# A network of ten stages on one core: expert weights in 2 MB slots with 16 KB per partition, and two more megabytes loaded before the expert stage

## The chip, the cores and the metric

The kernel runs on one core of one Trainium2 chip. It is one program that computes three network blocks one after the other. The metric is the device time of one execution in microseconds, as the median of several runs. All matrices are float32.

## The reference, cut to what matters

The change touches only the mixture of experts in the second block. There are 256 tokens of width 1024 and 32 experts; each token goes to four of them. Cut to the arithmetic, an expert does this with its tokens:

```python
gu = xb @ w1[e] + b1[e]                       # 1024 -> 2048
gate = jnp.minimum(gu[:, :D_FF_2], SWIGLU_LIMIT)
up = jnp.clip(gu[:, D_FF_2:], -SWIGLU_LIMIT, SWIGLU_LIMIT)
act = (up + 1.0) * gate * jax.nn.sigmoid(SWIGLU_ALPHA * gate)
return (act @ w2[e] + b2[e]) * g[:, None]     # 1024 -> 1024
```

`w1` is `w_expert_in_2`, 8 MB an expert, and `w2` is `w_expert_out_2`, 4 MB an expert. Thirty-two experts are 384 MB of weights, more than half of the 721 MB that the whole program moves. Every expert's weights are read once.

## The kernel before

The expert stage is `moe_body`. It runs from about 685 us to 1692 us of the trace. It works through 16 pairs of experts (`pair`, L1697), the two experts side by side: a matmul has up to 64 tokens of one expert as its stationary side and fills half of the PE array's columns, and the other expert's matmul fills the other half. In one pair, PE does these things in order: four products with `w_expert_in` (two column halves `c`, each with a gate and an up `part`; tile `xg` holds the gathered tokens), and between and behind them the gated activation on DVE and ACT (`gm`, `um`), transposed into `aT`; then two products with `w_expert_out` (`c` = 0, 1), each copied to `ye` by ACT and added to the tokens' sums by four matmuls `ogT,ye`. Matmuls `oh,hh` and `oh,hl` gather the next pair's tokens into a bank, from which ACT copies `xg`; they are placed among the products of the current pair. A pair ends with its second `ogT,ye` group.

So a pair has six groups of weights, o0 to o5, of 4 MB each: 2 MB of either expert. Before the change a group is four loads of 1 MB, in the order lower half of the rows of expert 0, of expert 1, upper half of expert 0, of expert 1. Each load is one contiguous megabyte in memory, 8 KB for each of 128 partitions. `slot` (L1526) takes the buffers in rotation: eight 1 MB buffers of the pool `ring2` (tag `raw2`), then four of `self.ring` (tag `raw`), which all stages share. A load can be issued when PE has done the last matmul with what its buffer held before.

All of these loads are issued by SP, in order. If one waits for its buffer, everything behind it on SP waits too. The hardware's queue holds what was issued already; eight completion lanes (DMAHW0 to DMAHW7 in the order's rows) are used in turn, and a load also waits for the previous one of its lane.

Two further things share the stage. Before it, during the memory attention, `prefetch` loads the first 15 MB of pair 0: twelve into the ring, and three (`SPARE`, group indices 4, 13, 14) into buffers that are idle then. These loads stand on SP among those of `w_mem_q` and `w_mem_o`. And in pairs 3 to 6 (`FILL` = 3), PE does a product for the next block with 1 MB of `l_mem_wkv`, the fill: 48 matmuls. The fill's megabyte takes a buffer of tag `raw` at the end of the pair before, is split there by ACT (CAST to `whi`) and DVE (`wlo`), and its buffer is free when the split is done. The source of that product, `mem_3`, is loaded by GpSimd at the start of the stage into a buffer of its own (`kv0`), and its norm is worked out after pair 1.

After pair 7 stands a loop for experts with more than 64 tokens (`more`, L1785); here it runs zero rounds, but all engines pass through its branch.

The order of instructions on each engine is not written out. A planner goes through the code with modelled times of engines and loads, and decides from them what goes next: where the gather's matmuls are placed among a product's, and where the fill's split stands on ACT and DVE. When the sizes and waits of the loads change, that order changes too.

## Time and profile before

| | |
|---|---|
| median of three runs | 2866.47 us (2864.63 to 2870.25) |
| the profiled execution, its own time | 2866.68 us |
| its span in the trace | 2864.9 us |
| expert stage in the trace | about 685 to 1692 us |
| PE busy over the span | 96% |
| DMA over the whole span | 721 MB, mean 252 GB/s |

The median and the profiled execution differ by 0.2 us. Outside the expert stage, the DMA engines are about half busy. Inside it they move 421 GB/s in most slices, while PE's busy share is 94% and more. PE's busy time is modelled from pipelined matmuls, so a high share alone doesn't tell whether PE or the loads set the pace. That is read from the stretches of one pair: the length of a pair from end to end, the DMA share in it, and what PE waits for.

### The profile page before, as it was taken

Reading aid. Unit: us, or ns where it says so; the run is one execution under the profiler, and the core shown is the slowest. Engines: PE = TensorE matmul, PEld = TensorE weight load, DVE = VectorE, ACT = ScalarE, POOL = GpSimd, SP = SyncE. Lnnn points to the kernel's source line nnn. Section 1 sums busy time; section 2 is a strip of 40 time slices with the busy share of each in tenths; the row PEclk is TensorE's granted clock in tenths of the full one; section 3 lists DMA queues with packets and bytes.
Section 4 is the critical chain, followed back from the end, with each engine's and each line's share of the span. In section 5 each row is a group of like instructions: output and inputs, shape, how many; then the busy total and the mean of one; then the engine's idle time right before and its main releaser. Section 6 shows DMA issues by size and latency. Waiting matters only on the chain.

```text
span 2864.9 us, 45348 instructions
## 1 busy us (share of the span) xinstructions
PE 2751.9 (96%) x19079; PEld 2166.1 (76%) x19079; DVE 1340.0 (47%) x2203; ACT 1081.8 (38%) x1770; POOL 88.0 (3%) x153
## 2 busy tenths in 40 slices
PE   7999999999999999899999999999999999999999
PEld 7899999997434444333334359999899989999999
DVE  5566877564111111111101145569765555676655
ACT  4454655653011111000000034456654444566543
POOL 0000000010000000000000000001100000000000
PEclk9999999999999999999999999999999999999999
DMA  8446555475998999899999987654445585654453
GB/s 214 139 154 198 191 177 177 148 264 216 379 405 362 371 370 421 363 421 421 421 421 421 421 294 198 200 160 147 135 148 181 173 207 188 193 164 146 149 180 130
DMA packets 305638, 721.16 MB, mean 252 GB/s; under 512 B 13925, under 2 KB 233493, under 8 KB 256402
## 3 DMA queue, kind: packets, MB, share of 16 engines
q1 hardware_dynamic: 302194, 707.85, 67.0%
q0 software_dynamic: 2944, 10.08, 2.5%
q8 instruction: 152, 2.49, 0.4%
q14 instruction: 60, 0.49, 0.0%
q10 hardware_dynamic: 288, 0.25, 0.0%
HBM read 710.00 MB, written 8.13 MB: 251 GB/s over the span
## 4 chain that ended last, share of the span: by engine, by line
PE 49%; DVE 4%; ACT 2%; DMA 2%; issue 1%; ACTq 0%; DVEq 0%
PE bank L115 49%; DMA raw<-l_ffn_wd 2%; DVE wlo L115 1%; ACT whi L115 1%; DVE um L115 1%; DVE att_s L115 1%; DVE xnl L115 1%; ACT xnh L115 0%; ACT att_s L115 0%; ACT ye L115 0%; DVE att_nm L115 0%; DVE xT L115 0%; ACT sq L115 0%; ACT ma_p L115 0%; DVE rs_t L115 0%
## 5 line engine op out<-in xcount | busy, mean ns | idle before, releaser
L115 DVE TENSOR_TENSOR wlo<-raw,whi 128x1024 fp32r<-128x1024 f32 x560 | 687.4, 1230 | 534.5 <-ACT whi L115 531.3
L115 PE MATMUL bank<-xnh,whi 128*128 128x256 f32 x2960 | 847.3, 287 | 6.8 <-ACT xnh L115 6.8
L115 PE MATMUL bank<-xnl,whi 128*128 128x256 f32 x2960 | 842.1, 285 | 6.8 <-DVE xnl L115 6.8
L115 PE MATMUL bank<-xnh,wlo 128*128 128x256 f32 x2960 | 839.3, 284 | 2.2 <-DVE wlo L115 2.2
L115 ACT CAST whi<-raw 128x1024 fp32r<-128x1024 f32 x560 | 584.0, 1046 | 678.5 <-PE bank L115 618.8
L115 PEld LDWEIGHTS bank<-xnh,whi 128*128 128x128 f32 x2960 | 568.7, 192 | 14.9 <-ACT xnh L115 6.8
L115 PEld LDWEIGHTS bank<-xnl,whi 128*128 128x128 f32 x2960 | 568.9, 192 | 11.7 <-DVE xnl L115 10.9
L115 PEld LDWEIGHTS bank<-xnh,wlo 128*128 128x128 f32 x2960 | 568.9, 192 | 3.0 <-DVE wlo L115 2.8
L115 PE MATMUL bank<-raw,xg 128*64 128x512 f32 x2024 | 476.6, 595 | 9.7 <-DMA raw<-w_expert_in 9.6
L115 PEld LDWEIGHTS bank<-raw,xg 128*64 128x64 f32 x2024 | 162.2, 137 | 291.1 <-issue 267.9
L115 PE MATMUL bank<-hh,whi 128*128 128x256 f32 x880 | 248.9, 284 | 10.8 <-ACT whi L115 10.8
L115 PE MATMUL bank<-raw,aT 128*64 128x512 f32 x1024 | 254.1, 597 | 0.7 <-ACT aT L115 0.7
L115 PE MATMUL bank<-hh,wlo 128*128 128x256 f32 x880 | 249.8, 284 | 0.9 <-DVE wlo L115 0.9
L115 PE MATMUL bank<-hl,whi 128*128 128x256 f32 x880 | 250.0, 284 | 0.2 <-DVE hl L115 0.2
L115 PEld LDWEIGHTS bank<-hh,whi 128*128 128x128 f32 x880 | 169.0, 193 | 11.2 <-ACT whi L115 11.2
L115 PEld LDWEIGHTS bank<-raw,aT 128*64 128x64 f32 x1024 | 75.7, 136 | 130.7 <-issue 126.6
L115 PEld LDWEIGHTS bank<-hh,wlo 128*128 128x128 f32 x880 | 169.4, 193 | 1.5 <-DVE wlo L115 1.5
L115 PEld LDWEIGHTS bank<-hl,whi 128*128 128x128 f32 x880 | 169.6, 193 | 0.6 <-DVE hl L115 0.6
L115 PE MATMUL bank<-whi,xnh 128*128 128x256 f32 x544 | 160.4, 295 | 7.1 <-ACT whi L115 7.1
L115 PE MATMUL bank<-wlo,xnh 128*128 128x256 f32 x544 | 155.9, 287 | 2.8 <-DVE wlo L115 2.8
L115 PE MATMUL bank<-whi,xnl 128*128 128x256 f32 x544 | 155.6, 286 | 0.5 <-DVE xnl L115 0.5
L115 DVE TENSOR_SCALAR gm<-bank 128x512 f32<-128x512 f32 x32 | 22.1, 692 | 261.4 <-PE bank L115 261.4
(379 smaller groups left out, 2689.1 us busy)
## 6 DMA issues: line engine op xcount, KB each, us to landing
raw<-w_expert_in SPq DMA_DIRECT2D x253, 1024.0 KB, 17.9
raw<-w_expert_out SPq DMA_DIRECT2D x128, 1024.0 KB, 16.9
raw<-l_ffn_wg SPq DMA_DIRECT2D x44, 1024.0 KB, 5.4
raw<-l_ffn_wu SPq DMA_DIRECT2D x44, 1024.0 KB, 5.4
raw<-l_ffn_wd SPq DMA_DIRECT2D x44, 1024.0 KB, 4.9
raw<-w_in SPq DMA_DIRECT2D x32, 1024.0 KB, 5.3
raw<-l_w_in SPq DMA_DIRECT2D x26, 1024.0 KB, 5.2
raw<-w_up SPq DMA_DIRECT2D x22, 1024.0 KB, 5.1
```

Of the source, the lines that this page charges most:

```text
L115: return real(*a, **k)
```

## The change

An expert's part of a group, 2 MB, becomes one load with 16 KB for each partition (`whole`). `ring2` now has four buffers of 2 MB in place of eight of 1 MB, so the room is the same. Two groups of three go there. Every third group is loaded as four halves of 1 MB (`half`) into the four shared `raw` buffers; a half reads 8 KB out of each partition's 16 KB. The weights lie in memory in another order (`layout`), made beforehand: each expert's part is contiguous, 16 KB a partition. A group is asked for once, at its first half of the rows (`get`), and both experts' loads of 2 MB must have landed before its first matmul.

`prefetch` loads 17 MB instead of 15. The two further megabytes go into a buffer `extra` in the stage's work pool, and into the buffer of `mem_3`, which is free until then; the load of `mem_3` moves behind pair 0, still on GpSimd's queue. What remains of o4 is loaded in the stage (`rest`).

```diff
--- before.py
+++ after.py
@@ -307,8 +307,7 @@
     pass
 
 
-RING2 = 8
-SPARE = (4, 13, 14)
+RING2 = 4
 LOOP = 7
 FILL = 3
 MIXAT = 5
@@ -1513,8 +1512,6 @@
         es, pool, ring2 = st.moe_es, st.moe_pool, st.ring2
         st.kv_es = ExitStack()
         st.kv0.own = nc.pool(st.kv_es, name="kv0")
-        st.kv0.raw = st.kv0.own.tile([128, KB, T], F32, tag="kv0", name="mem0")
-        nc.gpsimd.dma_start(out=st.kv0.raw, in_=A["mem_3"].rearrange("(k p) t -> p k t", p=128))
         wk = nc.pool(es, 1, name="moew", side="right")
         st.kv0.pool = Instead(wk, hn_q="gm", hn_q2="um", hn_ms="hn_ms")
         new = lambda name, shape, dt=F32: pool.tile(shape, dt, name=name)
@@ -1523,19 +1520,28 @@
         WI, WO = A["w_expert_in_2"], A["w_expert_out_2"]
         self.slots = 0
 
-        def slot(W):
-
-            p, tag = (self.ring, "raw") if self.slots % (4 + RING2) >= RING2 else (ring2, "raw2")
-            self.slots += 1
-            t = p.tile([128, 4, 512], F32, tag=tag, name=tag)
+        def half(W, pool=self.ring, tag="raw"):
+
+            t = pool.tile([128, 4, 512], F32, tag=tag, name=tag)
             nc.sync.dma_start(out=t, in_=W)
             return [t[:, k] for k in range(4)]
 
-        def spare(W, whole):
-            if whole:
-                t = self.ops.tile([128, 4, 512], F32, tag="xnl", name="spare")
-                nc.sync.dma_start(out=t, in_=W)
-                return [t[:, k] for k in range(4)]
+        def whole(W, k0=0):
+
+            t = ring2.tile([128, KB, 512], F32, tag="raw2", name="raw2")
+            nc.sync.dma_start(out=t[:, k0:], in_=W[:, k0:])
+            return [t[:, k] for k in range(KB)]
+
+        def slot(Ws):
+
+            self.slots += 1
+            if self.slots % 3:
+                return [whole(W) for W in Ws]
+            a = [half(W[:, :4]) for W in Ws]
+            b = [half(W[:, 4:]) for W in Ws]
+            return [a[e] + b[e] for e in range(2)]
+
+        def spare(W):
             r = []
             for k, tag in ((0, "whi"), (2, "wlo")):
                 t = self.wsp.tile([128, 2, 512], F32, tag=tag, name="spare")
@@ -1556,13 +1562,25 @@
         def order(n):
 
             es = (2 * n, 2 * n + 1)
-            return ([WI[e, 2 * part + c, kh] for c in range(2) for part in range(2) for kh in range(2) for e in es]
-                    + [WO[e, c, kh] for c in range(2) for kh in range(2) for e in es])
+            return [[WI[e, 2 * part + c] for e in es] for c in range(2) for part in range(2)] + [
+                [WO[e, c] for e in es] for c in range(2)]
 
         def prefetch(n):
 
-            for i, W in enumerate(order(n)[:4 + RING2 + len(SPARE)]):
-                ahead.append(spare(W, i == SPARE[0]) if i in SPARE else slot(W))
+            o = order(n)
+            for i in range(3):
+                ahead.append(slot(o[i]))
+            a, b = o[3]
+            b0 = half(b[:, :4], wk, "extra")
+            c0 = half(o[4][0][:, :4], st.kv0.own, "kv0")
+            a0 = half(a[:, :4], self.ops, "xnl")
+            a1, b1 = spare(a[:, 4:]), spare(b[:, 4:])
+            ahead.append([a0 + a1, b0 + b1])
+
+            def rest():
+                self.slots += 1
+                return [c0 + whole(o[4][0], 4)[4:], whole(o[4][1])]
+            ahead.append(rest)
 
         prefetch(0)
 
@@ -1700,7 +1718,15 @@
             if fill:
                 self.issue(fill)
             og, xg = next(got)
-            get = over_slot if over else lambda W, e: ahead.pop(0) if ahead else slot(W)
+            got2 = []
+
+            def get(Ws, kh):
+                if over:
+                    return [over_slot(W[:, 4 * kh:4 * kh + 4], e) for e, W in enumerate(Ws)]
+                if kh == 0:
+                    w = ahead.pop(0) if ahead else slot(Ws)
+                    got2[:] = w() if callable(w) else w
+                return [w[4 * kh:4 * kh + 4] for w in got2]
             aT, ye = ((self.ops, "xnl"), (self.ops, "xnh")) if over else ((self.wsp, "whi"), (self.wsp, "wlo"))
             aT = aT[0].tile([128, KB, 128], F32, tag=aT[1], name="aT")
             late = []
@@ -1720,7 +1746,7 @@
                     bk = begun.pop(0) if begun else biased(n, c, part)
                     bks.append(bk)
                     for kh in range(2):
-                        w = [get(WI[e0 + e, 2 * part + c, kh], e) for e in range(2)]
+                        w = get([WI[e0 + e, 2 * part + c] for e in range(2)], kh)
                         for k in range(4):
                             for e in range(2):
                                 mm(out=bk[64 * e:64 * e + 64, :], lhsT=xg[:, 4 * kh + k, e], rhs=w[e][k],
@@ -1767,7 +1793,7 @@
             for c in range(2):
                 bk = self.bank()
                 for kh in range(2):
-                    w = [get(WO[e0 + e, c, kh], e) for e in range(2)]
+                    w = get([WO[e0 + e, c] for e in range(2)], kh)
                     for k in range(4):
                         for e in range(2):
                             mm(out=bk[64 * e:64 * e + 64, :], lhsT=aT[:, 4 * kh + k, 64 * e:64 * e + 64],
@@ -1810,6 +1836,10 @@
             done = pair(i, got.pop(i), y, between=None if i in (LOOP, 15) else lambda: prepare(i + 1),
                         fill=st.kv0.order[i - FILL] if FILL <= i < FILL + 4 else None)
             yield NOW
+            if i == 0:
+                kv = st.kv0
+                kv.raw = kv.own.tile([128, KB, T], F32, tag="kv0", name="mem0")
+                nc.gpsimd.dma_start(out=kv.raw, in_=A["mem_3"].rearrange("(k p) t -> p k t", p=128))
             if i == LOOP:
                 more()
                 prepare(i + 1)
@@ -2286,7 +2316,7 @@
         a = np.asarray(inputs[name])
         a = a if a.ndim == 2 else a[0]
         if name in ("w_expert_in_2", "w_expert_out_2"):
-            a = a.reshape(32, 2, 4, 128, -1, 512).transpose(0, 4, 1, 3, 2, 5)
+            a = a.reshape(32, 8, 128, -1, 512).transpose(0, 3, 2, 1, 4)
         arrays[name] = f(a)
     return arrays
```

The first place is on SP at the end of a pair ahead of a fill: the pair's last expert loads, the fill (`l0_mem_wkv`), and the next pair's first loads. Names in brackets are the counters that a load waits for: load lanes (DMAHW), or the engine that last used the buffer. Before:

```order
L115 DMA raw_8414<-w_expert_out_2 128x2048 [waits DMAHW2_49,PE_49]
L115 DMA raw_8446<-l0_mem_wkv_3 128x8x256 [waits DMAHW3_49,PE_49]
L115 DMA raw_8499<-w_expert_in_2 128x2048 [waits DMAHW4_49,PE_49]
L115 DMA raw_8501<-w_expert_in_2 128x2048 [waits DMAHW5_49,PE_49]
L115 DMA raw_8511<-w_expert_in_2 128x2048 [waits DMAHW6_49,DMAHW2_49,PE_49]
L115 DMA raw2_8513<-w_expert_in_2 128x2048 [waits DMAHW7_49]
...
L115 DMA raw_8588<-w_expert_in_2 128x2048 [waits DMAHW7_49,DVE_49]
```

After:

```order
L115 DMA raw2_8358<-w_expert_out_2 128x4096 [waits DMAHW2_49,PE_49]
L115 DMA raw2_8360<-w_expert_out_2 128x4096 [waits DMAHW3_49,PE_49]
L115 DMA raw_8400<-l0_mem_wkv_3 128x8x256 [waits DMAHW4_49,PE_49]
L115 DMA raw_8453<-w_expert_in_2 128x2048 [waits DMAHW5_49,PE_49]
L115 DMA raw_8455<-w_expert_in_2 128x2048 [waits DMAHW6_49,PE_49]
L115 DMA raw_8457<-w_expert_in_2 128x2048 [waits DMAHW7_49,PE_49]
L115 DMA raw_8459<-w_expert_in_2 128x2048 [waits DMAHW4_49,DMAHW0_49,DVE_49]
L115 DMA raw2_8480<-w_expert_in_2 128x4096 [waits DMAHW1_49,PE_49]
L115 DMA raw2_8482<-w_expert_in_2 128x4096 [waits DMAHW2_49,PE_49]
```

Before, two 1 MB loads follow the fill, and the third waits for PE's use of the pair's last load (lane DMAHW2), with eight loads behind it. After, three 1 MB loads follow it, and the fourth waits for DVE's use of the fill's own megabyte (lane DMAHW4).

The second place is on ACT at the same end of the pair, from the pair's first `ye` copy to its last `xg` copies; `whi` is the fill's split. Before:

```order
L115 COPY ye_8694<-bank_8695 128x512 [waits PE_49]
L115 COPY xg_8761<-bank_8762 128x256 [waits PE_49,Activation_49]
L115 COPY ye_8694<-bank_8725 128x512 [waits PE_49]
L115 CAST whi_8866<-raw_8755 128x1024 [waits DMAHW4_49]
L115 CAST whi_8870<-raw_8755 128x1024
L115 COPY xg_8761<-bank_8772 128x256 [waits PE_49]
```

After:

```order
L115 COPY ye_8640<-bank_8641 128x512 [waits PE_49]
L115 COPY xg_8699<-bank_8700 128x256 [waits PE_49,Activation_49]
L115 COPY xg_8699<-bank_8710 128x256 [waits PE_49]
L115 CAST whi_8800<-raw_8693 128x1024 [waits DMAHW5_49]
L115 CAST whi_8804<-raw_8693 128x1024
L115 COPY ye_8640<-bank_8667 128x512 [waits PE_49]
L115 COPY xg_8699<-bank_8720 128x256 [waits PE_49]
```

The split moved ahead of the second `ye` copy, and behind a second `xg` copy.

The third place is on PE in pair 13, the second `w_expert_out` group, from the first `ogT,ye` group to the second. Before:

```order
L115 MATMUL bank<-ogT,ye 128x256 x4
L115 MATMUL bank<-oh,hh 128x128
...
L115 MATMUL bank<-oh,hh 128x128
L115 MATMUL bank<-raw_16202,aT 64x512
L115 MATMUL bank<-raw_16200,aT 64x512
...
L115 MATMUL bank<-raw_16202,aT 64x512
L115 MATMUL bank<-oh,hl 128x128
L115 MATMUL bank<-oh,hh 128x128
L115 MATMUL bank<-raw_16212,aT 64x512
L115 MATMUL bank<-oh,hl 128x128
```

After:

```order
L115 MATMUL bank<-ogT,ye 128x256 x4
L115 MATMUL bank<-oh,hh 128x128
...
L115 MATMUL bank<-oh,hl 128x128
L115 MATMUL bank<-oh,hh 128x128
L115 MATMUL bank<-raw_15984,aT 64x512
L115 MATMUL bank<-raw_15982,aT 64x512
...
L115 MATMUL bank<-raw_15984,aT 64x512
L115 MATMUL bank<-oh,hl 128x128
...
L115 MATMUL bank<-ogT,ye 128x256 x4
```

Before, the gather's matmuls stand as 3, 2, 10 and 4 among weight matmuls in runs of 7, 1 and 7. After, 17 of them stand together ahead of a run of 15 weight matmuls, and 4 behind it. The same change of order is in pairs 2 and 8 to 14.

## Rows read from the trace of the kernel before

**Rows 1.** Windows by pair: us, busy time (instructions) by engine, PEclk, DMA share, GB/s.

```profile
870.00:938.00 68.00, 62.08 (x309) 29.06 (x307) 9.96 (x16) 10.04 (x16) 0.00 (x0) 1.00 0.94 386
...
1333.00:1393.00 60.00, 56.85 (x268) 23.66 (x267) 6.84 (x13) 4.94 (x10) 0.00 (x0) 1.00 1.01 421
```

**Rows 2.** PE's timeline at pair ends 2, 6, 8, 14: start, us, engine, operation.

```profile
868.10 1.99 PE L115 MATMUL bank<-ogT,ye 128*128 128x256 f32 x8
...
1140.96 1.99 PE L115 MATMUL bank<-ogT,ye 128*128 128x256 f32 x8
...
1270.93 1.99 PE L115 MATMUL bank<-ogT,ye 128*128 128x256 f32 x8
...
1631.15 1.99 PE L115 MATMUL bank<-ogT,ye 128*128 128x256 f32 x8
```

**Rows 3.** PE's waits, 871 to 1143: engine, line <- awaited: us, times, longest.

```profile
PE bank L115 <- DVE um L115: 11.5, 8, 1.6
PE bank L115 <- DMA raw<-w_expert_in: 9.6, 9, 1.3
```

**Rows 4.** PE's waits, 685 to 871, the longest of five rows.

```profile
PE bank L115 <- DVE um L115: 2.4, 2, 1.6
```

**Rows 5.** PE's waits, 1274 to 1692, the longer of two rows.

```profile
PE bank L115 <- DVE um L115: 16.7, 14, 1.6
```

**Rows 6.** Tile whi, 900 to 925: count, ns min/median/max, first and last start.

```profile
L115 PE MATMUL bank<-whi,xnl x16: 279/283/283, 911.9 to 917.3; 128*128 128x256 f32 x16
```

**Rows 7.** SP's timeline around the end of pair 2 (two windows).

```profile
841.15 7.03 SPq L115 DMA_DIRECT2D raw<-w_expert_in  x2
...
867.45 5.04 SPq L115 DMA_DIRECT2D raw<-w_expert_in  x9
```

**Rows 8.** Windows at the ends of pairs 2 to 5, columns as in rows 1.

```profile
855.00:870.00 15.00, 14.92 (x74) 8.33 (x72) 0.81 (x5) 5.29 (x9) 0.00 (x0) 1.00 0.24 87
930.00:940.00 10.00, 9.92 (x58) 6.16 (x55) 2.36 (x2) 3.59 (x6) 0.00 (x0) 1.00 0.48 190
1000.00:1010.00 10.00, 9.92 (x55) 6.03 (x56) 2.85 (x4) 3.97 (x7) 0.00 (x0) 1.00 0.55 208
1070.00:1075.00 5.00, 4.92 (x25) 3.00 (x21) 1.06 (x1) 2.75 (x4) 0.00 (x0) 1.00 0.30 108
```

**Rows 9.** Timeline of ACT and DVE at the end of pair 2.

```profile
867.46 0.59 ACT L115 COPY ye<-bank 128x512 f32<-128x512 f32 x1 [3.98 <-PE bank L115]
...
869.63 2.00 ACT L115 CAST whi<-raw 128x1024 fp32r<-128x1024 f32 x2
...
870.71 2.36 DVE L115 TENSOR_TENSOR wlo<-raw,whi 128x1024 fp32r<-128x1024 f32 x2 [10.73 <-ACT whi L115]
```

**Rows 10.** PE's timeline, second half of pair 10.

```profile
1370.51 7.09 PE L115 MATMUL bank<-raw,aT 128*64 128x512 f32 x32
...
1379.91 0.41 PE L115 MATMUL bank<-oh,hh 128*128 128x128 f32 x1
...
1384.42 1.07 PE L115 MATMUL bank<-raw,aT 128*64 128x512 f32 x2
1385.42 0.33 PE L115 MATMUL bank<-oh,hl 128*128 128x128 f32 x1
...
1386.68 3.65 PE L115 MATMUL bank<-raw,aT 128*64 128x512 f32 x14
...
1391.01 1.35 PE L115 MATMUL bank<-ogT,ye 128*128 128x256 f32 x5
```

**Rows 11.** DMA queue 1 in 1275 to 1650: packets, MB, share of 16 engines.

```profile
q1 hardware_dynamic: 21643, 157.59, 101.1%
```

**Rows 12.** The same in 1700 to 2800, after the expert stage.

```profile
q1 hardware_dynamic: 143852, 182.64, 51.3%
```

**Rows 13.** Window 727 to 762 in pairs 0 and 1, columns as in rows 1.

```profile
727.00:762.00 35.00, 34.92 (x171) 17.84 (x171) 2.32 (x7) 3.25 (x7) 0.00 (x0) 1.00 0.82 334
```

**Rows 14.** PE's waits, 585 to 690, all rows.

```profile
PE bank L115 <- DVE xnl L115: 0.6, 2, 0.3
```

## The prediction, made before the changed kernel ran

> **What bounds the kernel now.** Only the expert stage changes, so I read that stage and leave the rest of the time alone. First come the windows, one for each pair of experts. In a pair with no extra product the DMA engines are full (share 1.01, 421 GB/s) and PE is busy 56.85 of 60 us; in a pair with a fill (a 1 MB load of the next network's weights and its product) the DMA share is 0.94, in a longer stretch [rows 1]. The starts of the last ogT group of the pairs give the period: 868.10 to 1140.96 is four fill pairs, 68.2 us each; 1270.93 to 1631.15 is six pairs of 60.04 us [rows 2]. Then the list of waits, by engine. PE waits for weights only in the fill pairs: 9.6 us in nine waits [rows 3]; before them its list has five rows, from pair 8 on two (the longer of these: 14 waits for DVE), and all are short waits for DVE and ACT [rows 4, 5]. So the steady pairs are bound twice: PE's own order takes 60.04 us and the DMA queue is full for the same time. One that gets faster alone brings nothing. As a check on the 9.6: the product is sixteen triples of matmuls, whose last ones start from 911.9 to 917.3, 0.36 us apart: 5.8 us [rows 6]; 60.04 + 5.8 = 65.8, and four pairs at 68.2 are 9.6 us over that.
>
> Where these 9.6 us come from is seen on SP. The fill takes one of four raw buffers, so the fourth raw load after it (counting it) must wait until PE has used the last megabyte of the pair. SP issues two loads at 841.15, then nothing more goes out until 867.45, when nine come in a burst [rows 7]. The queue runs dry meanwhile: DMA share 0.24 in 855-870, 0.48 in 930-940, 0.55 in 1000-1010, 0.30 in 1070-1075 [rows 8]. That is 11.4 + 5.2 + 4.5 + 3.5 = 24.6 us of idle DMA.
>
> **Term A, the wait behind the fill: -7.5 us.** The change leaves the four-buffer ring to the halved groups alone. After the fill come three halves whose buffers were used a group and more earlier, and only the fourth waits, now for the fill's split (CAST on ACT, wlo on DVE) instead of the pair's last matmul. Two things follow. One more megabyte is queued ahead of the wait: 1.049 MB at 421 GB/s is 2.49 us. And the split now stands before the pair's last ye copy on ACT; before, ye started at 867.46 and the CASTs at 869.63 [rows 9]. In the changed order the split can begin when the gather's first two xg copies are done, with 15 matmuls of the last group still to run, 7.1 us by a run of 32 records (16 matmuls) in the trace [rows 10]; two CASTs in 2.00 us and the second wlo behind them (two in 2.36 us) end some 3.4 us later, so the buffer comes free about 3.5 us sooner than the last matmul did. Together 6.0 us. Taken from the four stretches: 11.4 - 6.0 = 5.4 us remain, the other three vanish; 19.2 of 24.6 us, or 78%, and 78% of 9.6 us is 7.5. Bounds: 0 (the wait only changes its name) and 9.6 (no wait left). The freed PE time is not taken back by DMA: 25 MB per fill pair at 2.49 us are 62.3 us, under PE's 65.8.
>
> **Term B, the steady pairs: -3.9 us.** Two effects, of which the smaller counts.
> PE's order: in the last WO group the gather for the next pair no longer cuts the weights' run into 7, 1 and 7 matmuls; it stands in one piece ahead of a run of 15. Experts share the array by column halves, and a run that stops on the odd one leaves a half unused: one record pair alone takes 1.00 us (1384.42 to 1385.42). From the first gather to ogT the stretch is 11.1 us now (1379.91 to 1391.01) [rows 10]. The new order has 21 gather matmuls there at 0.126 us (ten took 1385.42 to 1386.68) and 15 weight matmuls, at most 7.1 us: 9.75 us. PE saves about 1.3 us a pair, bounds 1.0 and 1.6.
> DMA: two thirds of the bytes go in 16 KB runs. The trace has no run that long. Queue 1 has 21643 packets for 157.59 MB at 101.1% of 375 us on 16 engines, 280 ns for 7281 B [rows 11]; after the expert stage it has 143852 packets for 182.64 MB at 51.3% of 1100 us, 62.8 ns for 1270 B [rows 12]. A line through the two gives 17 ns a packet and 0.0362 ns a byte: two packets of 8 KB 627 ns, one of 16 KB 610, 2.7% less. Sixteen of a pair's 24 MB are 39.8 us, so 1.1 us at most; the other bound is nothing (the bytes themselves may be the limit). I take the middle, 0.55, because the line joins packets of mixed sizes and is extended beyond its end. PE's 1.3 us covers it. Seven pairs (8 to 14; 15 gathers nothing, so its order on PE is as before) make 3.9 us, bounds 0 and 7.7.
> The Trainium skill, "DMA: Bandwidth & Descriptors", section "Why small descriptors are slow", puts a fixed 3 cycles on a packet that moves 32 B a cycle: 259 cycles for 8 KB, 515 for 16 KB, a gain of 0.6% and not 2.7%. By it term B would be an estimated 1.6 us.
>
> **Term C, PE's order elsewhere: -2.5 us.** Pair 2 has the same rearrangement and no wait for DMA [rows 4]: 1.3 us. Pairs 1 and 3 to 6 lose one break between kinds of matmul each. The middle piece's surplus over a full slot (1.00 against 7.1/8 = 0.89) is 0.1 us and a gather run's start costs about as much; 0.25 us each, 1.2 in all. Bounds 1 and 3.
>
> **Edits costed at nothing.** The two further megabytes before the stage land earlier, but PE waits for no weights before 871 [rows 4], and the ring fills up anyway: in 727-762 the DMA share is 0.82, 6.3 us idle [rows 13]. More data ahead is only more idle time later. If the queue were the bound, they would be worth 2 x 2.49 = 5.0 us; I keep that as an end. mem_3's load now falls between pairs 0 and 1, in the same idle time; it is needed after pair 1, some 50 us later; without that cover it costs 2.5 us. The 2 MB loads that stand between those of w_mem_q and w_mem_o put up to one megabyte more ahead of two of them, 2.5 us each if uncovered; but PE's only wait in 585-690 is 0.6 us for DVE [rows 14]. At the end, both experts' 2 MB must have landed before the last 16 matmuls, not the last half: 3.5 us at most, if DMA were last there. SP's fewer issues free no one.
>
> **Sum.** 7.5 + 3.9 + 2.5 = 13.9 us. The profiled execution took 2866.68 us (span 2864.9), 0.2 above the median of the runs: 2852.8, say 2853.
>
> **Rivals.**
> (1) Nothing moves. The wait on the split lasts as long as that on the last matmul, since the split cannot start before its load has landed and ACT is in order; and 16 KB runs gain nothing. Term C alone remains, perhaps 1 to 3 us more: 2861 to 2866. For it: ACT's CAST must still pass the xg copies, whose PE work is at the end of the pair. Against it: the extra megabyte in the queue alone covers half of three of the four stretches.
> (2) The queue is the bound all through, and all is credited: 9.6 + 7.7 + 3 + 5 = 25.3 us, 2841. For it: DMA share 1.01 in the steady pairs. Against: PE without any wait for DMA there [rows 5].
> (3) Slower, by coarser pieces. Before, PE starts a group when the first 2 of its 4 MB are there and uses them in 3.5 us while the rest lands; now both experts' full 2 MB must be there. Wherever PE has caught up with DMA, the group ends up to 3.5 us later. Place: after each of the four fill breaks, at the loop after pair 7 and in every pair if the stage is paced by DMA. Price: five places are 17.5 us, which with term C and without A and B is 2866.7 + 17.5 - 2.5 = 2882. It decides as soon as weights land less than 3.5 us before use; with three such places A and C are eaten up. The trace speaks against it in the steady pairs (no wait for a load in 418 us), for it in the fill pairs, which do wait.
>
> **How the numbers follow.** Forecast 0.60; rival 1 0.16; rival 2 0.10; rival 3 0.14. A measurement of this kernel tells some 0.2% (5.7 us) from no change. Faster by more than that: 0.60 + 0.10 = 0.70; within: 0.16; slower: 0.14. The range runs from 2841 (rival 2) to 2869 (rival 1 and the mildest of rival 3), leaving out most of rival 3 and a little below.
>
> **What would show it.** A: SP's blocked stretch at the ends of pairs 2 to 5 short, the DMA share there near 1 (some idle left at the first), PE's 9.6 us of waits down to 2 and a fill pair at 66 us. B: steady pairs at 59.5 us with a DMA rate of 423 to 427 GB/s and one run of 15 matmuls; at 60.0 with 421 GB/s, long runs gain nothing; at 58.7, DMA was not the bound. C: pair 2 at 61.8. Wrong would be: PE waits for raw2 loads in steady pairs (rival 3), a rate below 421 GB/s (each percent costs 0.6 us a pair), or changes outside the expert stage.

## The result: 2846.5 us, 19 us less, and the profile after

| | before | after |
|---|---|---|
| median | 2865.55 us | 2846.52 us (2845.49 to 2851.73, 4 runs) |
| ratio of the runs | | 0.9934, 95% interval 0.9923 to 0.9946 |
| profiled execution, span | 2864.9 us | 2849.9 us |

Timed again, beside the experiments, the changed kernel took 2849.43 us, ratio 0.9942 (0.9926 to 0.9957). The profiled execution is the longest of the first four runs, so its span shows 15.0 us of the 19.0.

The windows by pair, of the changed kernel (columns as in rows 1). They answer to [rows 1]; both kinds of pair are shorter, so the windows are.

```profile
868.00:934.00 66.00, 63.53 (x326) 30.18 (x324) 9.21 (x15) 9.53 (x17) 0.00 (x0) 1.00 1.00 414
...
1320.00:1379.00 59.00, 55.85 (x270) 23.57 (x268) 6.84 (x13) 5.03 (x10) 0.00 (x0) 1.00 1.01 424
```

PE's timeline at the ends of pairs 2, 6, 8, 14 and 15, of the changed kernel; the first four answer to [rows 2].

```profile
867.17 1.99 PE L115 MATMUL bank<-ogT,ye 128*128 128x256 f32 x8
...
1125.62 1.99 PE L115 MATMUL bank<-ogT,ye 128*128 128x256 f32 x8
...
1254.05 1.99 PE L115 MATMUL bank<-ogT,ye 128*128 128x256 f32 x8
...
1605.65 1.99 PE L115 MATMUL bank<-ogT,ye 128*128 128x256 f32 x8
...
1668.08 1.92 PE L115 MATMUL bank<-ogT,ye 128*128 128x256 f32 x8
```

The differences of these starts give the stretches:

| stretch | before | after | difference |
|---|---|---|---|
| pairs 3 to 6 (fills) | 272.86 us | 258.45 us | -14.4 |
| pairs 7 and 8 (loop) | 129.97 us | 128.43 us | -1.5 |
| pairs 9 to 14 | 360.22 us | 351.60 us | -8.6 |
| pair 15 | 59.04 us | 62.43 us | +3.4 |
| from there to the end of the span | 1174.7 us | 1181.8 us | +7.1 |

The end of pair 2 is 0.9 us earlier. Pair 15 of the kernel before ends with a group at 1690.19. So the expert stage gained about 22 us, and 7 of them were lost behind it.

The waits of PE in the fill pairs (862 to 1130) and from pair 9 on (1258 to 1680), of the changed kernel (engine, line <- awaited: us in total, times, longest). They answer to [rows 3] and [rows 5].

```profile
PE bank L115 <- DVE um L115: 9.6, 8, 1.6
```

```profile
PE bank L115 <- DVE um L115: 16.8, 14, 1.6
...
PE bank L115 <- ACT sq L115: 1.6, 2, 1.4
```

No wait for a load is left in either. The queue at the ends of pairs 2 to 5, of the changed kernel (columns as in rows 1); it answers to [rows 8].

```profile
855.00:870.00 15.00, 14.92 (x85) 9.48 (x84) 3.17 (x7) 7.45 (x11) 0.00 (x0) 1.00 0.75 294
...
918.00:930.00 12.00, 12.00 (x64) 6.05 (x59) 2.36 (x2) 3.22 (x5) 0.00 (x0) 1.00 0.97 364
982.00:994.00 12.00, 12.00 (x65) 6.05 (x62) 2.36 (x2) 3.22 (x5) 0.00 (x0) 1.00 0.92 341
1046.00:1059.00 13.00, 13.00 (x69) 6.46 (x66) 2.36 (x2) 3.54 (x5) 0.00 (x0) 1.00 0.94 351
```

The idle time of DMA there is 15 x 0.25 + 12 x 0.03 + 12 x 0.08 + 13 x 0.06 = 5.9 us, 3.8 of it at the first place. It was 24.6.

### The profile page after: what moved, and what is told of

Same layout as the page of the kernel before. It is cut to its first block, busy times and chain, and to the rows that moved or that the text cites. A ratio compares the mean times of both kernels' runs of the same rounds, so it can differ in the third digit from the quotient of the medians.

```text
span 2849.9 us, 45107 instructions
## 1 busy us (share of the span) xinstructions
PE 2738.2 (96%) x19079; PEld 2160.6 (76%) x19079; DVE 1340.7 (47%) x2203; ACT 1081.9 (38%) x1769; POOL 87.8 (3%) x153
## 4 chain that ended last, share of the span: by engine, by line
PE 47%; DVE 5%; DMA 3%; ACT 3%; issue 1%; SPq 0%; DVEq 0%; ACTq 0%
PE bank L115 47%; DVE wlo L115 1%; DMA raw<-l_ffn_wu 1%; DMA raw<-l_ffn_wd 1%; ACT whi L115 1%; DMA raw<-w_expert_out 1%; DVE um L115 1%; DVE att_s L115 1%; DVE xnl L115 1%; ACT xnh L115 0%; ACT att_s L115 0%; ACT ye L115 0%; DVE xT L115 0%; DVE att_nm L115 0%; ACT sq L115 0%
## 5 line engine op out<-in xcount | busy, mean ns | idle before, releaser
L115 PE MATMUL bank<-xnh,whi 128*128 128x256 f32 x2960 | 848.2, 287 | 17.7 <-ACT whi L115 10.8
L115 PEld LDWEIGHTS bank<-xnl,whi 128*128 128x128 f32 x2960 | 569.8, 193 | 12.4 <-DVE xnl L115 10.8
L115 PE MATMUL bank<-raw,xg 128*64 128x512 f32 x2016 | 463.3, 595 | 0.0
L115 PEld LDWEIGHTS bank<-raw,xg 128*64 128x64 f32 x2016 | 155.9, 137 | 283.7 <-issue 283.6
L115 PE MATMUL bank<-raw,aT 128*64 128x512 f32 x1016 | 244.1, 599 | 0.1
```

Of the source, the lines that this page charges most:

```text
L115: return real(*a, **k)
```

## The experiments

All of them ran with the kernel before beside them on the same chip; its medians there were 2865.9 to 2866.5 us.

**The changed kernel again.** No edit.

> The changed kernel once more, on the chip of the three kernels beside it. The first profile showed steady pairs of 58.60 us, fill pairs of 64.45 to 64.89 us, the end of the expert stage 22.2 us earlier than before and the end of the program only 15 us earlier. If the loss behind the expert stage is a fixed collision (PE waiting 10.8 us for one load of l_ffn_wu beside a 2.3 MB store of POOL), it is there again, and the time is 19 us under before, give or take 3. If it was chance, PE's wait there is back at some 5 us.

2849.43 us. Pairs 1 to 15 repeat within 0.2 us (58.60 in pairs 9 to 14, 62.3 in pair 15), and so does the loss behind the stage: PE waits 11.0 us there. It is no chance. What SP waits for at the end of pair 2 (846 to 874) is in its list of waits:

```profile
SPq L115 <- DVE wlo L115: 8.6, 1, 8.6
```

The wait for the fill's split (DVE wlo, 8.6 us) has taken the place of the one for PE, as forecast, and the queue runs less dry meanwhile: the DMA share in 855 to 870 is 0.75, where it was 0.24 [rows 8].

**The fill's own buffer, in the kernel before.**

```diff
             if fill:
+                fill.raw = wk.tile([128, 2048], F32, tag="fillraw", name="fillraw")
+                for k in range(0, fill.kb, fill.kb // fill.pieces):
+                    self.fetch(fill.raw, fill.W, fill.k0 + k, fill.kb // fill.pieces, fill.c0, fill.ncols, k)
                 self.issue(fill)
```

> The kernel before, with one change: the fill's megabyte goes into a 1 MB buffer of its own, not into the ring of four raw buffers. Theory (the wait behind the fill is the cause of the 9.6 us): SP is no longer blocked at the ends of pairs 2 to 5, the 24.6 us of idle DMA there vanish, PE's waits for weights in pairs 3 to 6 go from 9.6 us to under 1, the fill pairs from 68.2 to 65.8 us; the time falls by 9 to 10 us. Rival (fill pairs got shorter through PE's order; the wait on SP only shifts where the queue lags): fill pairs stay within 1 us of 68.2, the time falls by less than 4 us. Steady pairs stay at 60.04 by both.

2853.68 us, ratio 0.9957 (0.9943 to 0.9970). PE's timeline at the ends of pairs 2, 6, 8 and 14:

```profile
864.55 1.99 PE L115 MATMUL bank<-ogT,ye 128*128 128x256 f32 x8
...
1123.58 1.99 PE L115 MATMUL bank<-ogT,ye 128*128 128x256 f32 x8
...
1253.85 1.99 PE L115 MATMUL bank<-ogT,ye 128*128 128x256 f32 x8
...
1614.08 1.99 PE L115 MATMUL bank<-ogT,ye 128*128 128x256 f32 x8
```

The fill pairs took 259.03 us, 13.8 less than before; pairs 9 to 14 still take 360.23, and no wait for weights is left in the fill pairs. So the wait behind the fill is what made the fill pairs longer, and this one buffer gives 12.2 us, two thirds or more of what the change gives.

The list of waits had put 9.6 us of the 13.8 down to loads. Another 1.9 us stood in it as waits for DVE, 11.5 us before [rows 3] and 9.6 now:

```profile
PE bank L115 <- DVE um L115: 9.6, 8, 1.6
```

The other 2.3 us are in rows that look busy: PE's busy time in the four pairs fell from 251.4 to 249.1 us. Part of that can be seen in pair 3. From the same weight matmul to the same `ident,um`, first in the kernel before, then here:

```profile
891.82 3.65 PE L115 MATMUL bank<-raw,xg 128*64 128x512 f32 x16
...
911.18 0.63 PE L115 MATMUL bank<-ident,um 128*128 128x128 f32 x4 [1.60 <-DVE um L115]
```

```profile
887.99 13.95 PE L115 MATMUL bank<-raw,xg 128*64 128x512 f32 x62
903.54 0.63 PE L115 MATMUL bank<-ident,um 128*128 128x128 f32 x4 [1.60 <-DVE um L115]
```

That is 19.36 against 15.55 us, 3.8 less, where the list had waits for loads of 0.51, 1.33 and 1.31. The order of PE in pairs 4 to 6 is the same in both kernels, in pair 3 it differs a little, so the order is at most a small part of it.

**PE's new order alone, in the kernel before.** The first half of the gather is written ahead of the last group, the rest of that group is ordered behind it, and the second half behind the group.

```diff
             for c in range(2):
                 bk = self.bank()
+                if c and between:
+                    with self.tc.issue_after(self.lastog.ins):
+                        between()
...
-                            mm(out=bk[64 * e:64 * e + 64, :], lhsT=aT[:, 4 * kh + k, 64 * e:64 * e + 64],
-                               rhs=w[e][k], start=kh == 0 and k == 0, stop=kh == 1 and k == 3)
+                            with (self.tc.issue_after(self.lastg.ins) if c and between and kh + k + e
+                                  else ExitStack()):
+                                self.lastraw = mm(
+                                    out=bk[64 * e:64 * e + 64, :], lhsT=aT[:, 4 * kh + k, 64 * e:64 * e + 64],
+                                    rhs=w[e][k], start=kh == 0 and k == 0, stop=kh == 1 and k == 3)
...
-            got[i] = ready(gather(i, pos))
+            g = gather(i, pos)
+            got[i] = rest(next(g), g)
```

> The kernel before with 1 MB loads as they were, but PE's order as in the changed kernel: the gather's first 16 matmuls in one piece behind the first ogT group, then the 16 weight matmuls of the last group in one piece. Theory of the prediction (the smaller of PE's and DMA's gain counts): DMA at 421 GB/s still needs 59.8 to 60.0 us a pair, so the pairs 9 to 14 stay at 60.0, and only pair 2 and the fill pairs gain: 2 to 4 us in all. Rival 1 (a stock of loaded weights pays the difference): pairs of 58.6 at first and 60.0 when the stock of some 3 us is used up, 4 to 7 us in all. Rival 2 (PE alone sets the pace): 58.6 in all six and 12 us or more in all.

2861.03 us, ratio 0.9981 (0.9972 to 0.9991). PE's timeline at the ends of pairs 8, 11, 12 and 14:

```profile
1265.83 1.99 PE L115 MATMUL bank<-ogT,ye 128*128 128x256 f32 x8
...
1441.77 1.99 PE L115 MATMUL bank<-ogT,ye 128*128 128x256 f32 x8
...
1502.78 1.99 PE L115 MATMUL bank<-ogT,ye 128*128 128x256 f32 x8
...
1622.28 1.99 PE L115 MATMUL bank<-ogT,ye 128*128 128x256 f32 x8
```

Pairs 9 to 11 took 175.94 us, 58.65 each. Then came 61.01, and two of 59.75. From pair 12 on PE waits for weights (1444 to 1685):

```profile
PE bank L115 <- DMA raw<-w_expert_in: 2.4, 3, 1.3
PE bank L115 <- DMA raw<-w_expert_out: 2.0, 4, 0.5
```

That is rival 1 of this experiment, and it is where the prediction's rule failed. PE's order takes 58.65 us, the loads at 421 GB/s need 59.8 (25.17 MB a pair). While weights lie loaded ahead, PE's pace counts. Each pair uses up 1.2 us of that stock, and when it is gone the loads' pace counts.

**8 KB runs in the changed kernel.** The weights lie in memory as before; loads, slots and PE's order are as in the changed kernel.

```diff
-            nc.sync.dma_start(out=t[:, k0:], in_=W[:, k0:])
+            nc.sync.dma_start(out=t[:, k0:].rearrange("p (h k) n -> p h k n", k=4), in_=W[k0 // 4:].rearrange("h p k n -> p h k n"))
...
-            a = a.reshape(32, 8, 128, -1, 512).transpose(0, 3, 2, 1, 4)
+            a = a.reshape(32, 2, 4, 128, -1, 512).transpose(0, 4, 1, 3, 2, 5)
```

> The changed kernel with the memory layout of before: the same 2 MB slots, the same number of loads and the same order on PE, but each 2 MB load reads two runs of 8 KB for a partition in place of one of 16 KB. If the run length makes the DMA faster, the rate goes from 425 back to 421 GB/s, the last landing of a pair moves 1.4 us a pair closer to its end instead of 0.6, the stock (15.7 us at pair 8, some 9.6 needed) is used up by pair 12, and the last pairs take 60 us: 3 to 5 us slower than the changed kernel. If run length does nothing and 2 MB a load is what helps, the rate stays at 425 and the time is that of the changed kernel within 1 us.

2856.58 us, ratio 0.9958 (0.9942 to 0.9974), by the medians 7 us above the changed kernel beside it, though the two intervals overlap. The window 1330 to 1440, first of the changed kernel run beside it, then of this one (columns as in rows 1):

```profile
1330.00:1440.00 110.00, 103.71 (x502) 43.64 (x499) 12.99 (x25) 9.53 (x20) 0.00 (x0) 1.00 1.01 426
```

```profile
1330.00:1440.00 110.00, 103.71 (x500) 43.62 (x497) 12.87 (x25) 9.46 (x19) 0.00 (x0) 1.00 1.01 421
```

426 against 421 GB/s. PE's timeline at the ends of pairs 8, 11, 12, 13, 14 and 15:

```profile
1252.50 1.99 PE L115 MATMUL bank<-ogT,ye 128*128 128x256 f32 x8
...
1428.31 1.99 PE L115 MATMUL bank<-ogT,ye 128*128 128x256 f32 x8
...
1487.91 1.99 PE L115 MATMUL bank<-ogT,ye 128*128 128x256 f32 x8
...
1549.03 1.99 PE L115 MATMUL bank<-ogT,ye 128*128 128x256 f32 x8
...
1607.64 1.99 PE L115 MATMUL bank<-ogT,ye 128*128 128x256 f32 x8
...
1673.45 1.93 PE L115 MATMUL bank<-ogT,ye 128*128 128x256 f32 x8
```

Pairs 9 to 11 are as in the changed kernel (58.60 each). Pair 12 takes 59.60, pair 13 61.12, pair 15 65.81 and not 62.3. PE's waits for loads from pair 12 on (1430 to 1675), and the window of pair 15:

```profile
PE bank L115 <- DMA raw<-w_expert_out: 2.6, 3, 1.0
```

```profile
1607.70:1673.50 65.80, 60.62 (x268) 25.50 (x269) 11.36 (x17) 9.09 (x17) 0.00 (x0) 0.92 0.94 371
```

So the run length is worth about 1.1% of the rate, some 0.65 us of a pair's 59.8, and that decides whether the stock lasts beyond pair 11. It doesn't explain all of the lost time. PE's granted clock in pair 15 is 0.92 (0.97 in the changed kernel, 1.00 in the kernel before), and in pair 13 it is 0.97. The run with the later store, below, has 16 KB runs and also 0.92 and 65.65 us in pair 15, so that pair's length isn't due to the run length alone. Where the parts of the weights lie in memory changed together with the run length; the two were not taken apart.

**Both single edits in the kernel before**, the own buffer and the new order.

> The kernel before with both single edits: the fill's own buffer, and the changed kernel's order on PE; loads stay 1 MB with 8 KB runs, and nothing more is loaded ahead. Theory (two causes that need each other: no wait behind the fill leaves a stock of 16 us at pair 8 where the new order alone had 11; the new order takes 58.65 us a pair and draws 1.2 us of stock a pair, and some 8 us must remain): pairs 9 to 14 all at 58.65, fill pairs 64 to 65, the expert stage 22 to 26 us shorter, the program 20 to 23 us faster than before, as much as the changed kernel or more. Rival (16 KB runs or 2 MB slots are needed for the gain): pairs go back to 59.8 to 60 from pair 11 or so on, the program is 15 to 17 us faster.

2843.37 us, ratio 0.9922 (0.9908 to 0.9936): as fast as the changed kernel, with 1 MB loads, 8 KB runs and 15 MB ahead. PE's timeline at the ends of pairs 8, 12, 14 and 15:

```profile
1250.41 1.99 PE L115 MATMUL bank<-ogT,ye 128*128 128x256 f32 x8
...
1485.00 1.99 PE L115 MATMUL bank<-ogT,ye 128*128 128x256 f32 x8
...
1603.82 1.99 PE L115 MATMUL bank<-ogT,ye 128*128 128x256 f32 x8
...
1665.30 1.99 PE L115 MATMUL bank<-ogT,ye 128*128 128x256 f32 x8 [0.71 <-ACT ye L115]
```

Four pairs at 58.65, then 118.82 us for pairs 13 and 14: the stock lasted one pair longer than with the new order alone, but not to the end. The changed kernel's gain is thus reached by other means; slots of 2 MB as such aren't needed for it. The two edits also help each other: pairs 9 to 14 gain 6.8 us here, 3.8 with the new order alone and nothing with the buffer alone.

**15 MB ahead in the changed kernel.** The two further megabytes are loaded inside the stage.

```diff
-            b0 = half(b[:, :4], wk, "extra")
-            c0 = half(o[4][0][:, :4], st.kv0.own, "kv0")
...
-            ahead.append([a0 + a1, b0 + b1])
+            ahead.append(lambda: [a0 + a1, half(b[:, :4]) + b1])
...
-                return [c0 + whole(o[4][0], 4)[4:], whole(o[4][1])]
+                return [whole(o[4][0]), whole(o[4][1])]
```

> The changed kernel without the two further megabytes ahead: 15 MB are loaded before the stage as in the kernel before, the missing halves inside the stage. Theory (PE waits for no load in pairs 0 to 2 and the ring fills up anyway): the same stock at pair 8 (15 to 16 us) and the same time within 2 us. Rival (what is loaded ahead is the stock that the steady pairs draw on): the stock at pair 8 is some 5 us less, 10 to 11 us, and two or three of the pairs 11 to 15 go to 59.2 us or more: 2 to 5 us slower than the changed kernel.

2852.31 us, ratio 0.9960 (0.9946 to 0.9973); the changed kernel's interval overlaps it. Pairs 9 to 14 take 58.60 us, none goes to 59.2, so the rival's loss of stock isn't there. PE waits for no load in pairs 0 to 2 either. Pair 2 is 2.4 us longer and pair 1 1.1 shorter, because ten matmuls of the gather stand in pair 2 and not in pair 1; PE's order in pair 0 is another too. Pair 15 is 1.8 us longer, at a granted clock of 0.95 and not 0.97, and pair 8 1.4 shorter. By the medians the two megabytes bring 3 to 6 us, which the intervals don't tell from nothing; in the trace the differences are in PE's order and its clock, and not in waits for loads. What they bring is left open.

**The store behind the stage, later.** Behind the expert stage POOL stores a 2.3 MB bias table, while the next stage's first weights are loaded. The trace of the changed kernel in 1683 to 1718 (queues: packets, MB, share of 16 engines; issues: count, KB, us to landing):

```profile
q0 software_dynamic: 688, 2.34, 56.9%
q1 hardware_dynamic: 2588, 3.31, 29.0%
...
scr_t<-toep_u POOLq DMA_DIRECT2D x1, 2304.0 KB, 36.8
raw<-l_ffn_wu SPq DMA_DIRECT2D x2, 1024.0 KB, 29.8
```

A megabyte of `l_ffn_wu` takes about 30 us to land beside it; in an undisturbed stretch it takes 5. PE's wait there, first of the kernel before, then of the changed kernel:

```profile
PE bank L115 <- ACT whi L115: 5.2, 1, 5.2
```

```profile
PE bank L115 <- ACT whi L115: 10.8, 1, 10.8
```

```diff
-        yield At(max(nc.ready(a) for a in (tab, oh)))
+        yield At(max(nc.ready(a) for a in (tab, oh)) + 60.0)
```

> The changed kernel with POOL's 2.3 MB store of the bias table some 60 us later in the stage behind the experts. Theory (PE's wait of 11 us there is for a load of l_ffn_wu that shares the DMA engines with this store while the ring of weights is still empty): the wait falls to under 2 us and the time by 8 to 11 us against the changed kernel. Rival (the load is late because the expert loads ended late, or the store costs the same wherever it stands): the wait of 10 us or a similar one is still there, the time changes by less than 3 us.

2845.00 us, ratio 0.9926 (0.9913 to 0.9940). The store moved by about 15 us only, and PE still waits 9.7 us for the split of a load beside it. The rival had that. Later in the same stage it costs about the same.

**Three orders at once.** The later store, the unbroken run of 16, and the next norm's sums behind the last pair's weights (`hold` is that pair's last weight matmul, behind which the sums are ordered).

```diff
+        st.norm.hold = self.lastraw
         for i in range(4):
             st.norm.add(i)
...
+                with net.tc.issue_after(self.hold.ins) if getattr(self, "hold", None) else ExitStack():
-                self.last = nc.tensor.matmul(
+                    self.last = nc.tensor.matmul(
```

> The changed kernel with three changes of order: the gather's first 16 matmuls in one piece ahead of all 16 weight matmuls of the last group, the sums of the next norm behind the last pair's weight matmuls and not ahead of them, and the bias store 60 us later. Theory: the steady pairs stay at 58.6 (the count of array slots is the same), pair 15 falls from 62.3 to 59 or 60 us, PE's wait behind the stage vanishes: 10 to 14 us faster than the changed kernel, 2834 to 2840 us. If only the store counts: 8 to 11 us faster. If neither does: within 2 us.

2846.45 us, ratio 0.9928 (0.9915 to 0.9942). Pair 15 fell to 59.2 us, as expected, and the stage ended 29 us earlier than before, but PE waits 10.4 us behind it, as in the changed kernel. The forecast of 10 to 14 us failed with that wait. In the trace some 5 us against the changed kernel remain at the end; the medians don't show them.

**The store at the start of the expert stage**, where [rows 13] and the stage's first windows showed idle DMA.

```diff
+        for _ in self.bias_even(st):
+            pass
         got = {0: gather(0, pos, True)}
...
-        raw = self.ring.tile([128, 2048], F32, tag="raw", name="raw")
...
+        raw = self.sm.tile([128, 2, T], F32, tag="sq", name="t5in").rearrange("p b t -> p (b t)")[:32]
```

The table's two small input loads move with the store, and no longer take one of the `raw` buffers.

> The changed kernel with POOL's 2.3 MB store of the bias table at the start of the expert stage, where the DMA engines are idle for a third of the time (share 0.65 in 685 to 752), and not behind the stage. Theory (the 11 us that PE waits behind the stage are for a load that shares the engines with that store): the wait is gone, the gain of 24 us at the end of the expert stage arrives at the end of the program, 8 to 12 us faster than the changed kernel, 2835 to 2841 us. Rival (the first loads of the next stage are late because expert loads end late): a wait of 8 us or more is still there, the time stays within 3 us. A third way: the store takes so much of the queue in pairs 0 and 1 that PE waits there for expert weights, and the gain is given back in pairs 1 to 3.

2839.18 us, ratio 0.9911 (0.9896 to 0.9927). Behind the stage PE waits for nothing. The rest of the program, from the last `ogT` group at

```profile
1674.27 1.93 PE L115 MATMUL bank<-ogT,ye 128*128 128x256 f32 x8
```

to the end of the span at 2837.7 takes 1163.4 us, 18 less than in the changed kernel. Some of it comes back, as the third way said: PE's waits in 685 to 870 now have

```profile
PE bank L115 <- DMA raw<-w_expert_out: 2.1, 2, 1.7
```

and pair 1 takes 62.0 us in place of 58.5; the stage ends 6.2 us later than in the changed kernel. The store costs less there than behind the stage.

**All orders with the early store:** the edit above, the unbroken run of 16 and the norm's sums behind the weights, in the changed kernel.

> The changed kernel with the early store, the unbroken run of 16 weight matmuls in the last group, and the next norm's sums behind the last pair's weight matmuls. Pair 15 at 59 us in place of 62.2, no wait behind the stage, steady pairs at 58.6: 11 to 15 us faster than the changed kernel, 2832 to 2838 us. If the last pair's gain is taken back by the next stage's loads, as with the store 60 us later: 8 to 11 us.

2834.68 us, ratio 0.9896 (0.9881 to 0.9911): the lowest median of all, 31.8 us under the kernel before. PE's timeline in the last pair:

```profile
1657.05 1.99 PE L115 MATMUL bank<-ogT,ye 128*128 128x256 f32 x8 [0.67 <-ACT ye L115]
1659.13 7.08 PE L115 MATMUL bank<-raw,aT 128*64 128x512 f32 x30
```

The sums (`og,sq`) now stand behind these 30 records. Pair 15 took 58.8 us.

**The same in the kernel before**, with the fill's own buffer.

> The kernel before (1 MB loads, 8 KB runs, 15 MB ahead) with the fill's own buffer, the new order on PE, the early store and the norm's sums behind the last pair's weights. Against before_buffer_and_order (2843 us) the wait of 4.7 us behind the stage vanishes; pair 15 stays near 61 us, because there the loads at 421 GB/s set the pace: 2836 to 2840 us. If 16 KB runs matter only where the stock is used up, it is 2 to 5 us slower than the changed kernel with the same three edits; if they matter everywhere, 7 us or more.

2836.69 us, ratio 0.9894 (0.9879 to 0.9909), not to be told from the kernel above. The pairs 13 to 15 are at 59.3, 59.6 and 60.8, where the 8 KB runs' rate shows.

## Why the prediction came out right, and where its steps were off

The forecast was 13.9 us, and 19.0 were measured: in the range and with the right sign, but that the sum came so near is in part luck, because errors of both signs met. In the traces the expert stage gained 22 us, and 7 were lost in a place that the prediction costed at nothing.

**Term A (-7.5 us): right in its mechanism, too small.** The wait on the split took the place of the wait on the last matmul; 3.8 us of idle DMA remained at the first end (forecast 5.4) and about 1 or less at each of the others (forecast 0). But the fill pairs gained 14.4 us, and the own buffer alone 13.8. The step that failed is the ceiling: I took PE's listed waits for loads, 9.6 us, as all that the late loads could cost. With them went 1.9 us of waits for DVE and 2.3 us in rows that look busy. The check on it failed with it. It put a fill pair without waits at 60.04 + 5.8 = 65.8 us; without waits it took 64.8 on average (its order on PE has one break fewer than a steady pair's). With the new order 58.60 + 5.8 = 64.4 comes near the 64.6 measured.

**Term B (-3.9 us): the rule "the smaller counts" failed.** Its two sizes were good. PE's order saves 1.44 us a pair (forecast 1.3), and the DMA rate went from 421 to 425 or 426 GB/s, some 0.65 us a pair (forecast 0.55; the line through the packets gave 1.1 as the upper end). But the pairs 9 to 14 went to 58.60, PE's own pace, and not to 59.5: 8.6 us in all, over the term's own upper bound of 7.7. A queue that is slower than PE is no bound while loaded weights lie ahead. The trace before showed that stock, and I did not ask for it: a pair's last load landed some 11 us ahead of the pair's last `ogT,ye` group. With the new order alone that lead falls from 9.1 us at pair 8 to 5.2 at pair 11, where PE begins to wait; in the changed kernel it falls from 13.8 us at pair 8 to 10.0 at pair 14, and PE doesn't wait. The runs with 8 KB and with the order alone show the stock being used up, and then the pace of the loads.

The rule of the Trainium skill that I weighed there ("DMA: Bandwidth & Descriptors", "Why small descriptors are slow": a fixed cost per packet) gave 0.6% for the whole loads. About 1.1% over all loads was measured, two thirds of the bytes in long runs, so some 1.6% for those. The measurement lies between the rule and the line through the packets (2.7%).

**Term C (-2.5 us).** Pair 2 gained 3.6 us, and pair 1 lost 1.9, since 16 matmuls of the gather moved from one to the other: 1.7 together, against 1.55 forecast for these two. The rest of the term is inside the fill pairs.

**What was costed at nothing.** What the prefetch brings is open: without its two further megabytes the traces show no wait for a load in pairs 0 to 2. PE waited for no load of `w_mem_q` or `w_mem_o`. The end of the stage did cost something, but not by the loads. In pair 15, the sums of the next norm now stand ahead of the last 15 weight matmuls, and PE waits for ACT's squares:

```profile
1652.88 1.99 PE L115 MATMUL bank<-ogT,ye 128*128 128x256 f32 x8 [0.67 <-ACT ye L115]
1656.25 1.05 PE L115 MATMUL bank<-og,sq 128*128 128x2 f32 x8 [1.38 <-ACT sq L115]
...
1658.56 8.78 PE L115 MATMUL bank<-raw,aT 128*64 128x512 f32 x30
```

In the windows 1653 to 1660 and 1660 to 1668 (columns as in rows 1) the granted clock is below 1 as well:

```profile
1653.00:1660.00 7.00, 5.36 (x30) 3.81 (x32) 4.00 (x7) 4.74 (x8) 0.00 (x0) 0.94 1.06 344
1660.00:1668.00 8.00, 8.00 (x34) 2.79 (x30) 1.42 (x2) 0.63 (x2) 0.00 (x0) 0.84 0.65 211
```

These windows hold a stretch of 3.4 us at 1.2 GHz (granted clock 0.50 in 1659.1 to 1662.5), behind PE's waits for the squares. With the sums behind the weights, the last pair is 3.5 us shorter, and its 30 records take 7.08 us in place of 8.78. The waits of 1.6 us and the 1.7 us that the records take longer make up most of that difference. The loss behind the stage was foreseen by no step: the order and the store of the next stage were never looked at. By the trace, one load fewer got through ahead of the store's transfers. The next load of `l_ffn` behind that of 1661 is issued only at 1676, and the loads of this stage follow each other at 5.8 us where nothing disturbs them, which is about what the wait grew by (from 5.2 to 10.8). That the store is what holds the load back is shown by the landing times beside it, in the changed kernel and with the later store, and by the run with the early store, though its edit moves the store's input loads as well. Ahead of the load of 1676 SP waits 14.7 us for DVE. DVE ends a split (`wlo`) just then, at 1676.30, and that split stands behind an operation of the next norm that had waited for PE. No run tests whether this is why the load is late.

**The rivals.** Rival 2 was right in that the upper ends of A and B were reached and passed in the stage, but for another reason: not the queue, PE set the pace. Rival 3, coarser pieces, did not come: the changed kernel has no wait for a load in any steady pair. But pieces of 2 MB need more stock: in the run with 8 KB runs PE waits in pair 12 at a lead of 9.4 us, where with 1 MB loads it waited at 5 to 6. Rival 1 falls with the fill pairs.

## What to carry to other kernels

Where two engines seem to bound a stage together, ask for the stock between them: the faster one sets the pace for as long as the buffers filled ahead last, and the gain of a faster consumer may be limited by the number of repeats and not by the slower rate. A wait that blocks a queue in order can cost more than its consumer's listed waits for the late data (13.8 us here against 9.6); the length of the stretch without it, measured by giving the blocked load a buffer of its own, is the better price. And when a stage ends earlier, look at what it now runs into: a gain of 22 us at the stage's end became 15 at the end of the span, through a transfer that was not part of the change.

## What the runs showed of the hardware

A pair's loads, two thirds of the bytes as 2 MB loads with 16 KB for each partition, ran at 426 GB/s; with two runs of 8 KB in place of each of 16 KB, and the same count of loads, at 421. A store of 2.3 MB from POOL (688 packets in 35 us) held 57% of the DMA engines' time, and 1 MB loads beside it took 25 to 35 us to land, where they otherwise take 5. PE's list of waits put 9.6 us down to loads where 13.8 were lost: 1.9 stood there as waits for DVE, and 2.3 were in rows that look busy, whose ends are modelled. And PE's granted clock fell to half for 3.4 us in pair 15 of the changed kernel, behind two short waits of 1.6 us in all.
